# The root of a layer norm on VectorE, other waiting rules of the planner, and 40 buffers for 37

## The chip, the cores and the metric

The kernel runs on one core of a Trainium2 chip. The metric is the device time of one execution in microseconds (us). The core's engines work side by side and wait for one another by semaphores: TensorE (PE, matrix products and transposes; PEld is its loading of weights), VectorE (DVE), ScalarE (ACT), GpSimd (POOL), and SyncE (SP), which issues the loads and stores.

## The reference

Two layers over 256 tokens of 1024 features. Each layer is a feed-forward block, a mixer, and a feed-forward block, and each of the six ends in a layer norm over the residual:

```
for l in range(DEPTH):
    x = _layer_norm(DN_ALPHA * x + 0.5 * _swiglu(x, ...pre...), ln_pre_g[l], ln_pre_b[l])
    mix = _hybrid_mixer(x, ...) if l % 2 == 0 else _ssd_mixer(x, ...)
    x = _layer_norm(DN_ALPHA * x + mix, ln_mix_g[l], ln_mix_b[l])
    x = _layer_norm(DN_ALPHA * x + 0.5 * _swiglu(x, ...post...), ln_post_g[l], ln_post_b[l])

def _layer_norm(x, g, b):
    xc = x - mean(x, -1); var = mean(xc * xc, -1)
    return xc * rsqrt(var + 1e-5) * g + b

def _swiglu(x, w_gate, w_up, w_down):
    return (silu(x @ w_gate) * (x @ w_up)) @ w_down
```

The hybrid mixer joins a gated delta rule and an mLSTM in chunks of 64 tokens, the SSD mixer is a chunked state-space model; both begin and end with large products with weights. All of it is float32.

## The kernel before, in words

**Products.** TensorE multiplies in float32r. For the precision of float32 each operand is kept as two tiles, `hi` (rounded) and `lo` (the rest), and a product is three matmuls (`mm3`, L676): hi by hi, hi by lo, lo by hi. Six such matmuls are one group of the planner (`mm3k`, L683).

**Weights.** `_wload` (L538) brings half a weight block of some 0.5 MB at a time: a load on SyncE into `raw`, a cast on ScalarE (`hi`), a subtraction on VectorE (`lo = raw - hi`). All three, and most large tiles of the mixers, take a buffer from the tag `m4`, which has NSLOT = 37 slots (L33, L61).

**Stages.** Six stages follow each other: feed-forward, hybrid mixer, feed-forward, feed-forward, SSD mixer, feed-forward. A stage reads the normalized `x`, transposed and split into `xh` and `xl`. The 256 tokens are two halves of 128. `close` (L670) ends a stage: for each half the last products (`tail`), then `layer_norm`. So the second half's tail is there to cover the first half's norm, and the next stage's first products with the first half are there to cover the second half's norm. There are five borders between stages and one end.

**The layer norm** of one half (`_layer_norm`, L650) is on VectorE: for each of two blocks of 512 columns `x<-acc,x` adds the residual and `st` takes statistics; `mv` joins them to mean and variance; a pass `x<-x,mv,lng` for each block; a pass `x<-x,rr,lnb` for each block, which needs the reciprocal root `rr`. Then `x_transpose` (L598): eight transposes on TensorE (`tr`), casts on ScalarE (`xh`), subtractions on VectorE (`xl`). The root is `rsqrt1` (L621), five operations on GpSimd: `rv` = variance + eps, `ry` = its power -0.5, two operations for `rh` and one for `rr`, which are a Newton step.

**The order.** Nothing is executed in the order of the program text. `Plan` records all operations; `rank` (L313) gives each a due time, worked back from the order of TensorE's operations, in which those within `hp()` (L499, the layer norm among them) are dated 600 operations earlier; `order` (L344) then plays the engines through with the costs of `_cost` and writes down for each engine a fixed sequence. The chip's engines follow their sequences and wait for semaphores. In each step the planner takes, of the operations that could start, the one that is due first; one that becomes ready only `t - t0` later is preferred to one ready now if it is due earlier by more than WAIT times that, and if the time is under FRAC of the other one's busy time (L413). A GpSimd operation that uses the port shared with VectorE can start only at `dve_port`, the planned end of the last such VectorE operation, and the other way round:

```
if q == "DVE" and o.port:
    t = max(t, pool_end)
if q == "POOL" and o.port:
    t = max(t, dve_port)
```

A VectorE operation uses the port in the plan when none of its operands is in PSUM and it has more than one column (L292 of `_cost`, `op.port`). The planned end counts LAG (84 ns on VectorE) beyond the time at which the engine is free for its next operation, and a result reaches the next VectorE operation 35 ns after that (HAND).

Of the kernel before, what the change touches and what calls it, by code (L numbers as in the profile page):

```python
# [12 lines left out]
F32 = mybir.dt.float32  # L13
F32R = mybir.dt.float32r
I32 = mybir.dt.int32
AF = mybir.ActivationFunctionType
ALU = mybir.AluOpType
AX = mybir.AxisListType

P = 128  # L20
# [6 lines left out]
ALPHA = (2 * DEPTH) ** 0.25  # L27
LN_EPS = 1e-5
# [1 line left out]
BIG = 1e30  # L30
CW = 260
WMAX = KB * CW
NSLOT = 37  # L33
RSQRT_MAGIC = 0x5F3759DF

C_NEG = 0
# [23 lines left out]

SB_SLOTS = {"m4": (NSLOT, WMAX), "m2": (6, 512), "m1": (6, 256), "tiny": (12, 16), "tiny96": (12, 96)}  # L61
PS_SLOTS = {"acc": 4, "gu": 2, "tr": 2}
# [119 lines left out]
class Plan:  # L182
# [83 lines left out]
    def _cost(self, op, method, a, k):  # L266
        q = op.engines[0]
        out = a[0]
        n = out.cols if isinstance(out, View) else 0
        if q == "PE":  # L270
            if method == "transpose":
                op.busy += 112
            else:
                load = 110 * a[1].cols / 128
                if a[1].dtype == F32R:
                    op.busy += max(load, .4375 * a[2].cols + 6)
                else:
                    op.busy += 2 * max(load, .834 * a[2].cols)
        elif q == "SP":
            op.busy = 330  # L280
            src = a[1]
            shape = out.shape if isinstance(out, View) else src.shape
            op.bytes = 4 * math.prod(shape)
            op.small = not (isinstance(src, bass.AP) and src.tensor.name.startswith("in_w") or "raw" in getattr(getattr(out, "buf", None), "name", ""))
        else:
            ins = [v for v in list(a[1:]) + list(k.values()) if isinstance(v, View)]
            wide = [v for v in ins if v.cols > 1]
            n = max([n] + [v.cols for v in wide])
            scal = sum(v.cols == 1 for v in ins) if n > 1 else 0
            ps = any(v.buf.psum for v in ins + [out])  # L290
            if q == "DVE":
                op.port = not ps and n > 1  # L292
                if method == "reciprocal":
                    t = 150 + 6.3 * n
                elif method == "tensor_tensor_scan":
                    t = 150 + 2 * n
                elif len(wide) < 2 and method.startswith("tensor_") and not ps:
                    t = 150 + .52 * n + 60 * scal
                else:
                    t = 150 + 1.045 * n + 50 * scal  # L300
                op.busy += t - LAG["DVE"]
            elif q == "ACT":
                op.busy += 180 + .85 * n + 60 * scal - LAG["ACT"] + (186 if "accum_out" in k else 0)
                f = a[2] if method == "activation" and len(a) > 2 else None
                if f in EXPS:
                    op.exps = True
                elif f == AF.Silu:
                    op.exps = False
            else:
                op.port = method != "memset"  # L310
                op.busy += 100 + .85 * n if method == "memset" else 930 if k.get("op") == ALU.pow else 250 + 2.25 * n
# [27 lines left out]
            o.prio = due[o]  # L339

    PE_DUE = False
    WAIT, FRAC = 2, .25

    def order(self):  # L344
        ops = self.ops
# [12 lines left out]
        free = {t: [(0.0, i) for i in range(SB_SLOTS[t][0] if t in SB_SLOTS else PS_SLOTS[t])] for t in line}  # L358
# [10 lines left out]
        def offer(o):  # L369
            for q in o.engines:  # L370
                cand[q].append(o)
# [5 lines left out]
        def start(o, q):  # L377
            t = max(ready[o, q], clock[q])
            if o.news:
                need = collections.Counter()  # L380
                for b in o.news:
                    if b.tag in line:
                        k = need[b.tag]
                        need[b.tag] += 1
                        before = 0
                        for e in line[b.tag]:
                            if e is b:
                                break
                            before += 1
                        if len(free[b.tag]) <= before:  # L390
                            return None
                        t = max(t, sorted(free[b.tag])[k][0])
            if q == "DVE" and o.port:
# [3 lines that stand above are left out]
            return t  # L397

        def switch(o, q):
            return 1300 if q == "ACT" and o.exps is not None and o.exps != table else 0  # L400

        while len(out) < len(ops):
            best = None
            for q in QUEUES:
                can = [(t, o) for o in cand[q] for t in (start(o, q),) if t is not None]
                if not can:
                    continue
                t0 = max(min(t for t, _ in can), clock[q] + 1)
                now = [(o.prio + 2 * switch(o, q), o.n, t, o) for t, o in can if t <= t0]
                mine = min(now)  # L410
                for p, n, t, o in sorted((o.prio + 2 * switch(o, q), o.n, t, o) for t, o in can if t > t0):

                    if p + self.WAIT * (t - t0) < mine[0] and t - t0 < self.FRAC * mine[3].busy:  # L413
                        mine = (p, n, t, o)
                        break
                mine = (None, mine[2] + switch(mine[3], q), mine[3])
                if mine and (best is None or mine[1] < best[0]):
                    best = (mine[1], q, mine[2])
            if best is None:
                raise RuntimeError("no operation can start: " + str([(q, [(o.n, o.calls[0][0], [(b.name, b.tag, line[b.tag][0].name if line.get(b.tag) else None, len(free.get(b.tag, ()))) for b in o.news]) for o in c[:4]]) for q, c in cand.items() if c]))  # L420
            t, q, o = best
            for e in o.engines:
                cand[e].remove(o)
            busy = o.busy
            if q == "POOL" and len(o.engines) > 1:
                busy = 150 + (o.busy - 66) * 2.2
            for b in o.news:
                if b.tag in line:
                    line[b.tag].remove(b)
                    s = min(free[b.tag])  # L430
                    free[b.tag].remove(s)
                    b.slot = s[1]
                    held[b] = 0.0
            clock[q] = t + busy
            end = t + busy + LAG[q]
            if q == "SP":
                first = max(dma, t + busy)
                dma = first + o.bytes / (200 if o.small else 410)
                end = dma + 2000
            if q == "ACT" and o.exps is not None:  # L440
                table = o.exps
            if o.port and q == "POOL":
                pool_end = end
            if o.port and q == "DVE":
                dve_port = end
            o.done, o.begun, o.on = end, t, q
            out.append(o)
            for u in users[o]:
                for e in u.engines:
                    r = t + 1 if o in u.after else end + HAND[q][e]  # L450
                    ready[u, e] = max(ready[u, e], r)
                left[u] -= 1
                if not left[u]:
                    offer(u)
            touched = {v.buf for _, a, k in o.calls for v in list(a) + list(k.values()) if isinstance(v, View)}
            for b in sorted(touched, key=lambda b: b.n):
                b.left -= 1
                if b in held:
                    held[b] = max(held[b], end + 60)
                    if not b.left:  # L460
                        free[b.tag].append((held.pop(b), b.slot))
# [18 lines left out]
class Net:  # L480
# [140 lines left out]
    def rsqrt1(self, v, eps, scale=None):  # L621
# [13 lines left out]
        G.tensor_mul(r, y, h)  # L635
        return r

    def ln_load(self, g, b):
        nc = self.nc
        gt = self.m4([P, D], nm="lng")  # L640
        bt = self.m4([P, D], nm="lnb")
        nc.sync.dma_start(gt, g.partition_broadcast(P))
        nc.sync.dma_start(bt, b.partition_broadcast(P))
        return gt, bt
# [5 lines left out]
    def _layer_norm(self, half, accs, scale, gb, last):  # L650
        nc = self.nc
        t = self.x[:, half, :]
# [4 lines left out]
            nc.vector.bn_stats(st[:, n, :], t[:, sl])  # L657
        mv = self.tiny([P, 2], nm="mv")
        nc.vector.bn_aggr(mv, st)
        r = self.rsqrt1(mv[:, 1:2], LN_EPS / ALPHA ** 2)  # L660
        for n in range(2):
            sl = slice(n * 512, n * 512 + 512)
            nc.vector.scalar_tensor_tensor(t[:, sl], t[:, sl], mv[:, 0:1], gb[0][:, sl], op0=ALU.subtract, op1=ALU.mult)
# [933 lines left out]
```

## Time and profile before

| what | us |
| --- | --- |
| median of 3 runs | 1186.47 (1184.49 to 1188.71) |
| the profiled execution | 1190.74 |
| its span, first to last instruction | 1189.0 |
| TensorE busy | 1132.2 |
| VectorE busy | 755.5 |
| ScalarE busy | 567.1 |
| GpSimd busy | 54.7 |

The profile is of one execution. A row of a table of stretches gives the busy time of an engine in the stretch, the number of its instructions in brackets, the granted TensorE clock as a share of full speed, the share of the DMA engines and GB/s. A row in order of time gives start, length, engine, line and operation, what it writes and reads with shapes and count, and in square brackets how long the engine was idle just before and what ended that. All operations stand under one line of the program, that of `emit`, so they are told apart by the names of their tiles.

### The profile page before, as it was taken

The page shows a single profiled execution, that of the slowest core. Times are in us where ns is not written, and L with a number is a line of the kernel's source. Part 1 is how long each engine was busy: PE and PEld are TensorE (multiplying, and loading weights), DVE is VectorE, ACT ScalarE, POOL GpSimd, SP SyncE. Part 2 cuts the span into 40 slices and gives each one's busy share as a digit, 9 for nine tenths or more (in the row PEclk, how much of TensorE's full clock was granted, in tenths as well). Part 3 has the DMA queues.
Part 4 walks back from the last instruction along what each step waited for, and adds up shares of the span by engine and source line. Part 5 has one row for each costly group of instructions (what it writes and reads, how often), then busy time and mean ns, then how long its engine had stood idle before and what let it go on. Part 6 is the DMA issues. An engine that isn't in the chain of part 4 may idle for free. (4 is left out here: it accounts for less than half of the span.)

```text
span 1189.0 us, 19681 instructions
## 1 busy us (share of the span) xinstructions
PE 1132.2 (95%) x8052; PEld 1051.8 (88%) x8052; DVE 755.5 (64%) x1208; ACT 567.1 (48%) x808; POOL 54.7 (5%) x113
## 2 busy tenths in 40 slices
PE   6999999898996999999899999899999997999996
PEld 6999998898985999999799999789999877999995
DVE  6745556698858744545854435578999866544534
ACT  6636453474423444534343434358778444443420
POOL 0000002000001000000100000010011100000001
PEclk9999999999998999999999999999999998999999
DMA  9656554657335454566454656355455654555510
GB/s 365 222 185 211 202 201 139 184 164 234 107 105 166 144 197 161 194 204 202 145 195 152 197 170 226 127 184 196 142 158 168 204 174 176 178 202 179 209 61 36
DMA packets 75811, 210.02 MB, mean 177 GB/s; under 512 B 13564, under 2 KB 26056, under 8 KB 75720
## 3 DMA queue, kind: packets, MB, share of 16 engines
q1 hardware_dynamic: 75720, 208.76, 52.6%
q8 instruction: 63, 1.03, 0.3%
q14 instruction: 28, 0.23, 0.1%
HBM read 204.23 MB, written 4.50 MB: 176 GB/s over the span
## 5 line engine op out<-in xcount | busy, mean ns | idle before, releaser
L477 DVE TENSOR_TENSOR lo<-raw,hi 128x1024 fp32r<-128x1024 f32 (+1 forms) x356 | 431.3, 1223 | 278.8 <-ACT hi L477 275.4
L477 ACT CAST hi<-raw 128x1024 fp32r<-128x1024 f32 (+1 forms) x356 | 370.8, 1049 | 356.9 <-DMA raw<-in_wgu 214.3
L477 PE MATMUL gu<-xh,hi 128*128 128x256 f32 x1216 | 342.0, 281 | 3.5 <-DVE hf L477 3.5
L477 PE MATMUL gu<-xh,lo 128*128 128x256 f32 x1216 | 342.1, 281 | 0.0
L477 PE MATMUL gu<-xl,hi 128*128 128x256 f32 x1216 | 342.1, 281 | 0.0
L477 PEld LDWEIGHTS gu<-xh,hi 128*128 128x128 f32 x1216 | 229.7, 189 | 5.1 <-DVE hf L477 3.7
L477 PEld LDWEIGHTS gu<-xl,hi 128*128 128x128 f32 x1216 | 229.7, 189 | 1.4
L477 PEld LDWEIGHTS gu<-xh,lo 128*128 128x128 f32 x1216 | 229.6, 189 | 0.0
L477 PE MATMUL acc<-hi,h 128*128 128x512 f32 x704 | 227.0, 395 | 0.0
L477 PEld LDWEIGHTS acc<-hi,h 128*128 128x128 f32 x704 | 132.1, 188 | 29.7 <-ACT h L477 0.4
L477 PE MATMUL acc<-lo,h 128*128 128x512 f32 x352 | 138.5, 394 | 0.0
L477 PE MATMUL acc<-xh,hi 128*128 128x256 f32 x320 | 93.9, 293 | 0.0
L477 PE MATMUL acc<-xl,hi 128*128 128x256 f32 x320 | 90.2, 282 | 0.0
L477 PE MATMUL acc<-xh,lo 128*128 128x256 f32 x320 | 90.1, 281 | 0.0
L477 PEld LDWEIGHTS acc<-lo,h 128*128 128x128 f32 x352 | 66.1, 188 | 14.0
L477 DVE TENSOR_TENSOR hf<-sg,gu 128x256 f32<-128x256 f32 (+1 forms) x100 | 38.4, 384 | 45.3 <-ACT sg L477 45.2
L477 ACT ACTIVATE sg<-gu 128x256 f32<-128x256 f32 (+1 forms) x100 | 35.4, 354 | 66.1 <-PE gu L477 65.8
L477 PE MATMUL acc<-hi,xl 128*128 128x260 f32 x224 | 64.4, 288 | 2.4 <-DVE xl L477 2.4
L477 PE MATMUL acc<-hi,xh 128*128 128x260 f32 x224 | 65.1, 291 | 0.5 <-ACT xh L477 0.5
L477 PE MATMUL acc<-lo,xh 128*128 128x260 f32 x224 | 64.2, 287 | 0.0
L477 PEld LDWEIGHTS acc<-xh,hi 128*128 128x128 f32 x320 | 60.7, 190 | 1.2 <-issue 0.7
L477 PEld LDWEIGHTS acc<-xl,hi 128*128 128x128 f32 x320 | 60.6, 189 | 0.7 <-issue 0.7
(267 smaller groups left out, 1439.6 us busy)
## 6 DMA issues: line engine op xcount, KB each, us to landing
raw<-in_wgu SPq DMA_DIRECT2D x176, 512.0 KB, 5.7
raw<-in_wd SPq DMA_DIRECT2D x88, 512.0 KB, 4.0
raw<-in_ssd_fm SPq DMA_DIRECT2D x24, 512.0 KB, 4.8
raw<-in_ssd_tm SPq DMA_DIRECT2D x16, 520.0 KB, 5.3
raw<-in_hyb_fm SPq DMA_DIRECT2D x16, 512.0 KB, 3.9
raw<-in_ssd_out SPq DMA_DIRECT2D x16, 512.0 KB, 4.8
raw<-in_hyb_tm SPq DMA_DIRECT2D x12, 520.0 KB, 4.8
raw<-in_hyb_out SPq DMA_DIRECT2D x8, 512.0 KB, 5.3
```

The source lines that it names most:

```text
L477: getattr(engines[o.on], method)(*map(real, a), **{x: real(v) for x, v in k.items()})
```

## The change

The root of the layer norms is computed by a new `rsqrt_dve` on VectorE, in nine operations on tiles of 128x1: the sum with eps (scaled), two integer operations for a first guess, three Newton steps of two operations each. The SSD mixer keeps `rsqrt1`. FRAC of the planner, .25 for all engines, becomes a table: .5 for VectorE, ScalarE and GpSimd, 0 for TensorE and SyncE, which then never wait for an operation that is due earlier. The planner's price of a float32r matmul is fitted anew (118.0 ns for 256 columns by either, 231.7 for 230.0 for 512). NSLOT goes from 37 to 40, and the space of SBUF set aside for DMA descriptors is made 512 bytes a partition. The loop that counts free slots is only left earlier.

```
-NSLOT = 37
+NSLOT = 40

-                    op.busy += max(load, .4375 * a[2].cols + 6)
+                    op.busy += max(load, .4441 * a[2].cols + 4.3)

-    WAIT, FRAC = 2, .25
+    WAIT = 2
+    FRAC = {"PE": 0, "DVE": .5, "ACT": .5, "POOL": .5, "SP": 0}

-                if p + self.WAIT * (t - t0) < mine[0] and t - t0 < self.FRAC * mine[3].busy:
+                if p + self.WAIT * (t - t0) < mine[0] and t - t0 < self.FRAC[q] * mine[3].busy:

+    def rsqrt_dve(self, v, eps):
+        V = self.nc.vector
+        T = lambda n, dt=F32: self.tiny([P, 1], dt, n)
+        ve, q, i, y = T("rv"), T("rq"), T("ri", I32), T("ry")
+        V.tensor_scalar(ve, v, eps, 2.0 ** 26, op0=ALU.add, op1=ALU.mult)
+        V.tensor_scalar(i, ve.bitcast(I32), 1, None, op0=ALU.logical_shift_right)
+        V.tensor_scalar(y.bitcast(I32), i, -1, RSQRT_MAGIC - 2 ** 31, op0=ALU.mult, op1=ALU.add)
+        for c in (3.0, 12.0, 768.0):
+            V.tensor_scalar(q, ve, y, y, op0=ALU.mult, op1=ALU.mult)
+            V.scalar_tensor_tensor(y, q, -c, y, op0=ALU.add, op1=ALU.mult)
+        return y

-        r = self.rsqrt1(mv[:, 1:2], LN_EPS / ALPHA ** 2)
+        r = self.rsqrt_dve(mv[:, 1:2], LN_EPS / ALPHA ** 2)

-    nc = bacc.Bacc("TRN2", target_bir_lowering=False, num_devices=1)
+    nc = bacc.Bacc("TRN2", target_bir_lowering=False, num_devices=1, dynamic_dma_scratch_size=512)
```

## Rows read from the trace of the kernel before

**Rows 1.** The page's first part: busy us, share of span, instructions by engine.
```profile
PE 1132.2 (95%) x8052; PEld 1051.8 (88%) x8052; DVE 755.5 (64%) x1208; ACT 567.1 (48%) x808; POOL 54.7 (5%) x113
```

**Rows 2.** Waits of TensorE over the span: total, times, longest.
```profile
PE tr L477 <- DVE x L477: 11.8, 4, 4.8
...
PE gu L477 <- DVE hf L477: 5.1, 2, 3.5
```

**Rows 3.** TensorE in the stretches of borders 1, 2, 3, about 745, borders 4, 5.
```profile
205.00:220.00 15.00, 11.12 (x80) 0.89 0.52 144
380.00:400.00 20.00, 15.99 (x106) 0.91 0.41 132
575.00:597.00 22.00, 18.30 (x121) 0.92 0.56 191
744.00:756.00 12.00, 8.51 (x60) 0.86 0.36 124
775.00:797.00 22.00, 19.12 (x126) 0.92 0.55 191
984.00:1006.00 22.00, 14.97 (x106) 0.84 0.30 107
```

**Rows 4.** TensorE in two single microseconds after border 3's first wait.
```profile
583.00:584.00 1.00, 1.00 (x6) 0.50 1.03 422
...
586.00:587.00 1.00, 1.00 (x10) 0.96 0.00 0
```

**Rows 5.** VectorE in order of time at border 3.
```profile
574.32 0.69 DVE L477 SCALAR_TENSOR_TENSOR x<-acc,x 128x512 f32<-128x512 f32 x1 [1.05 <-PE acc L477]
...
575.77 1.23 DVE L477 TENSOR_TENSOR lo<-raw,hi 128x1024 fp32r<-128x1024 f32 x1
...
579.93 0.21 DVE L477 BATCH_NORM_AGGREGATE mv<-st 128x2 f32<-128x12 f32 x1
580.18 1.41 DVE L477 SCALAR_TENSOR_TENSOR x<-x,mv,lng 128x512 f32<-128x512 f32 x2
581.51 1.28 DVE L477 TENSOR_TENSOR xl<-tr,xh 128x512 fp32r<-128x512 f32 x2
583.54 3.77 DVE L477 TENSOR_TENSOR lo<-raw,hi 128x1024 fp32r<-128x1024 f32 x3 [0.75 <-ACT hi L477]
...
587.42 3.49 DVE L477 TENSOR_TENSOR lo<-raw,hi 128x1024 fp32r<-128x1024 f32 x3
...
591.43 0.75 DVE L477 SCALAR_TENSOR_TENSOR x<-x,rr,lnb 128x512 f32<-128x512 f32 x1
```

**Rows 6.** GpSimd at border 3, the last of its five operations.
```profile
582.82 0.19 POOL L477 TENSOR_TENSOR rr<-ry,rh 128x1 f32<-128x1 f32 x1
```

**Rows 7.** GpSimd's last operation and VectorE's pass at border 5.
```profile
986.69 0.19 POOL L477 TENSOR_TENSOR rr<-ry,rh 128x1 f32<-128x1 f32 x1
...
996.64 1.41 DVE L477 SCALAR_TENSOR_TENSOR x<-x,rr,lnb 128x512 f32<-128x512 f32 x2
```

**Rows 8.** A root on VectorE in the hybrid mixer, first and twelfth operation.
```profile
365.17 0.17 DVE L477 TENSOR_SCALAR ri<-oss 128x8 int32<-128x8 int32 x1
...
367.39 0.17 DVE L477 TENSOR_TENSOR of<-ry,rq 128x8 f32<-128x8 f32 x1
```

**Rows 9.** VectorE busy in border 2's stretch and in the SSD mixer.
```profile
380.00:400.00 20.00, 18.91 (x26) 0.91 0.41 132
...
800.00:900.00 100.00, 91.78 (x193) 1.00 0.54 174
```

**Rows 10.** VectorE in the last layer norm.
```profile
1181.62 1.41 DVE L477 SCALAR_TENSOR_TENSOR x<-x,mv,lng 128x512 f32<-128x512 f32 x2
1184.49 1.42 DVE L477 SCALAR_TENSOR_TENSOR x<-x,rr,lnb 128x512 f32<-128x512 f32 x2 [1.46 <-POOL rr L477]
```

**Rows 11.** VectorE at border 2, between the first half's statistics and its root.
```profile
381.32 1.22 DVE L477 TENSOR_TENSOR lo<-raw,hi 128x1024 fp32r<-128x1024 f32 x1
```

**Rows 12.** ScalarE about 745.
```profile
746.06 1.06 ACT L477 CAST hi<-raw 128x1040 fp32r<-128x1040 f32 x1 [2.29 <-DMA raw<-in_ssd_tm]
```

More of the change, by code (lines that the diff above doesn't have):

```diff
@@ L385, in start @@
                         before = 0
+                        room = len(free[b.tag])
                         for e in line[b.tag]:
-                            if e is b:
+                            if e is b or before >= room:
                                 break
                             before += 1
-                        if len(free[b.tag]) <= before:
+                        if room <= before:
                             return None
```

## The prediction, on record before the result

> **What bounds the kernel now.** I read the shares first, then the list of what TensorE waited for, then tables of the stretches where it waited, then VectorE's order there. TensorE is busy for 1132.2 of 1189.0 us [rows 1], so time can come only out of its idle 56.8 us and out of what it runs at the lower clock. Of its waits the largest is for `x`, 11.8 us in four waits, by the transposes that open a stage [rows 2]. Two waits for `hf` come to 5.1 us.
>
> The five borders between stages stand in [rows 3], which I number in order of time: idle 3.9, 4.0, 3.7, 2.9 and 7.0 us, 21.5 us together. Each also shows a mean granted clock of 0.84 to 0.92. Single microseconds of border 3 show what that is: after a wait the engine is fully busy at a granted 0.50, the lower of its two levels (1.2 and 2.4 GHz), and some 3 us later it has the upper one again [rows 4]. (1 - 0.89) x 15 = 1.65 us is lost that way at border 1, and 1.8, 1.75 and 1.75 at borders 2, 3 and 4. At border 5 it is 3.5, of which I take 2.5, since part of that low clock falls into idle time.
>
> Why does TensorE wait? Border 3 on VectorE: the statistics `mv` of the second half are done at 580.14 [rows 5], GpSimd has the root `rr` at 583.01 [rows 6], but the pass that uses it (`x<-x,rr,lnb`) starts at 591.43 [rows 5]. In the 8.4 us between, VectorE runs six weight subtractions `lo`. They stand ahead of it in its queue, which is fixed by the program. The same shows at all five borders; the longest is border 5, with `rr` at 986.88 and the pass at 996.64 [rows 7]. So GpSimd isn't slow; the written order is wrong, and the code says why. The planner starts a GpSimd operation only after the last VectorE operation that shares the port with it has ended (L395), and counts 84 ns more for that end than for VectorE's next start. While subtractions are there, the five GpSimd steps starve in the plan, one coming in wherever VectorE has a gap or touches PSUM, and the pass is written behind the subtractions. On the chip the steps ran at once.
>
> **The root on VectorE, per layer norm.** Five GpSimd operations go, nine VectorE operations of 128x1 come. No row shows this size; the nearest are the existing root's operations on 128x8. From its first operation to the next operation after it there are eleven intervals in 367.39 - 365.17 = 2.22 us, 0.202 each [rows 8]. Nine cost 1.82 us. The bounds: 1.5 if only their busy time counted (0.17 each, [rows 8]), and 2.2 if each took as long as the `mv` operation (0.21, [rows 5]) and the same gap. I take 1.82, from the rows that are the same arithmetic. GpSimd took 2.87 us from `mv` to `rr`.
>
> The steps are VectorE's own now, so L395 no longer applies to them. A subtraction would have to get into the gap between two steps, 119 ns in the plan (84 of lag, 35 of hand-over); `hp()` dates the steps 600 operations earlier, and FRAC of .5 (before .25) of a subtraction's 1.14 us in the plan covers that gap. So the second half's `x` is done 1.82 + 4 x 0.71 = 4.7 us after `mv` (two passes take 1.41, [rows 10]): at border 3 at 584.8, if nothing comes between, against 592.8.
>
> **Borders 1, 3, 4, 5.** TensorE has the first half's matmuls to run meanwhile: at border 3 from the `xl` of 581.51 to the pass of 591.43 [rows 5], about 10 us. With `x` 6 to 9 us earlier the second wait is covered. The first wait at borders 3 and 4 is another thing, one for `xl` of the first half, which VectorE runs behind the second half's `mv` and its passes [rows 5]. Today the first half's `x` is late there through a subtraction of 1.23 us in front of its pass with `rr` [rows 5], and VectorE idles for 1.05 us before the second half's first accumulator [rows 5]. Out go these 2.28 us, in come 1.82: the pass ends some 0.4 us earlier, and its `xl` comes before the second half's last accumulator is read, not after. I leave 0.5 us of wait at each of these three borders. Gains: border 1 3.9 + 1.65 - 0.5 = 5.0; border 3 3.7 + 1.75 - 0.5 = 5.0; border 4 2.9 + 1.75 - 0.5 = 4.1. At border 5 the shorter of the two waits for `hf` (5.1 together, the longer 3.5, [rows 2]) stays, so 7.0 - 1.6 + 2.5 = 7.9. Sum 22.0.
>
> **Border 2** goes the other way. The tail is short there, both halves' statistics meet on VectorE, which is busy for 18.9 of 20 us [rows 9]. The first half's pass with `rr` already waits behind the second half's reads and statistics. One subtraction in front of it (1.22 us, [rows 11]) goes, nine steps (1.82) come, and some five steps of the second half (1.0) get in as well: 1.6 us later. The first half's `xl` has a planner's priority just behind the second half's first pass with `rr`, so one more pass (0.7) gets in front. Loss 2.5 us, between 0 and 4.
>
> The Trainium skill ("VectorE: DVE Perf Modes", Rules for kernel authors) says of chained VectorE operations to minimize their count. By that the change is wrong wherever VectorE is the late engine; border 2 is the place where that agrees with the trace, at the others VectorE's subtractions have time to spare. The same page (The TRN2 errata) gives about 150 cycles at 0.96 GHz as the fixed cost, an estimate of 1.41 us for nine and, at border 2 and the end, 0.8 us less in the sum; the rows' 1.82 decides.
>
> **The end.** The last layer norm has no subtraction before it. There GpSimd's root ran beside two passes of 1.41 us together, and the pass with `rr` follows 2.87 us after their start [rows 10]; now all is in one queue, 1.82 + 1.41 = 3.23. Loss 0.35, between 0 and 0.8.
>
> **The rest.** VectorE gets 12 x 1.82 = 22 us more, 755.5 [rows 1] to 777, 65% of the span: hidden except as said. FRAC of .5 for VectorE and ScalarE puts steps of the mixers ahead of a subtraction or cast by up to 0.57 us; of 0 for TensorE and SyncE a transpose or load no longer holds its engine idle, and may come one group of six matmuls (0.7 us) later. The new matmul price differs by 0.01 us at most. I cost these at nothing: TensorE's other idle time, 56.8 less 21.5 less some 18 at the start and the end, about 17 us, may go either way by some 6 us. Three more slots are one half weight (`raw`, `hi`, `lo`) more in flight. It pays where casts wait for a load: at 745 TensorE lost 3.5 us idle and 1.7 of clock [rows 3] with ScalarE's `hi` waiting 2.29 us for a load [rows 12]. I leave that out of the sum and put it in the range. The smaller scratch has no user in this trace: all loads of the page are issued on SyncE; nothing.
>
> **Sum.** -22.0 + 2.5 + 0.35 = -19.1 us. The profiled execution took 1190.74 us, 1.74 above its span, and stands 4.3 above the median of 1186.47. Taken off the profiled one it gives 1171.6; off the median 1167.4, which I forecast. A measurement of this kernel can tell about 0.3%, 3.6 us, from no change.
>
> **Rivals.** (a) *The first half's `xl` is left behind the second half's steps* at borders 1, 3 and 4 as well, if it becomes ready after `mv`. It would start 1.82 + 3 x 0.71 = 4.0 us after `mv`, not 1.4 [rows 5]: 2.6 more wait at borders 3 and 4, about 2.2 at border 1, clock loss stays. Gains become 1.1, -1.3, -2.1 and 7.9, less 2.85: 2.8 us, so 1184. For it: the planner's priorities. Against: in the plan as in [rows 5] the first half's `x` precedes the second half's last read by a little. Chance 0.13. (b) *Waits behind late loads go too*: 745 (5.2 us), the `hf` of border 5 (1.6), and border 2 without loss (2.5): 1158. For it one half weight more ahead; against, the plan counts with it too. Chance 0.15. (c) *The subtractions become late*, slower. VectorE is 91.8% busy from 800 to 900 [rows 9], and up to 0.57 us of waiting in front of a subtraction uses up the 8.2 us of slack at the fifteenth; I take 5 us lost. At the borders six subtractions go behind 4.7 us of layer norm; TensorE waits from the point at which a subtraction ends after its matmul is due, at most 4.7 at each of five, 23 us. Against the 22 gained: 1186 + 5 + 23 - 19 = 1195. Against it: no wait for `lo` is among TensorE's larger ones [rows 2], so there is a lead today. Chance 0.08. (d) *It doesn't do what it says*: other subtractions still stand ahead of the pass, or the wait moves to `hf` and weights: 1186. Chance 0.07. The forecast has 0.57.
>
> **Range and chances.** The forecast's own unknowns (border 2 by 2.5, small waits and mixers by 6, the steps by 0.4 at six places) give 1160 to 1177. To leave out no more than 2 in 10 it reaches to (b), less 3 of the mixers, at 1155 and to (a) at 1184. Faster: 0.57 + 0.15 + 0.06 of (a) = 0.78; within 0.3%: the other 0.07 of (a) and 0.05 of (d), 0.12; slower: (c) and 0.02 of (d), 0.10.
>
> **What would show it.** Right: at the borders the pass with `rr` starts within 3.5 us after `mv`, the wait of the transposes for `x` falls from 11.8 to under 4 us, TensorE's idle in these stretches from 21.5 to 8 or less, with its clock at 0.97 or more at borders 1, 3, 4; border 2 is worse; the last pass starts 3.2 us after `mv`. Wrong: TensorE waiting for `xl` over 2 us at borders 3 and 4 (a), waiting for `lo`, or VectorE over 95% from 800 to 900 (c), subtractions still ahead of the pass (d).

## The result and the profile after

The changed kernel takes 1157.26 us (median of 4 runs, 1153.92 to 1159.14) against 1187.59 for the kernel before: ratio 0.9741, 95% interval 0.9705 to 0.9778, or 30 us less. The forecast was 1167.4, 19.1 less, with 1155 to 1184. The profiled execution after took 1153.92 us with a span of 1152.1; it is the shortest of its four and the profiled one of before was on the long side, so the two traces differ by 36.9 us of span, more than the medians do.

First the page: the engines' shares, which answer [rows 1].

```profile
PE 1116.6 (97%) x8052; PEld 1040.2 (90%) x8052; DVE 775.4 (67%) x1316; ACT 571.9 (50%) x810; POOL 23.7 (2%) x53
```

TensorE idles for 35.5 us, 21.3 less than before. VectorE has 19.9 us more work. Then TensorE's waits, total, times and longest, as in [rows 2]:

```profile
PE tr L479 <- DVE x L479: 7.7, 7, 5.9
PE tr L479 <- DVE md L479: 3.5, 2, 2.6
PE tr L479 <- DVE xl L479: 1.7, 1, 1.7
PE tr L479 <- DVE hf L479: 1.1, 2, 0.8
```

5.9 of the 7.7 for `x` is one wait, at border 2; six others share 1.8. The stretches that answer [rows 3], placed by the `mv` of the second half: border 1, border 2 with the end of the mixer, border 3, the place that was at 745, borders 4 and 5.

```profile
205.00:220.00 15.00, 14.71 (x124) 1.00 0.73 224
350.00:395.00 45.00, 37.89 (x249) 0.92 0.48 154
563.00:585.00 22.00, 19.87 (x156) 1.00 0.62 205
732.00:744.00 12.00, 12.00 (x92) 1.00 0.50 166
755.00:777.00 22.00, 21.69 (x171) 1.00 0.65 222
957.00:979.00 22.00, 21.75 (x183) 1.00 0.57 201
```

The clock stays at its upper level at borders 1, 3, 4 and 5. To see border 2 whole, this is the same stretch of the kernel before, with the wait of the mixer in it:

```profile
355.00:400.00 45.00, 34.99 (x196) 0.89 0.45 148
```

Idle time plus the time lost by the clock, (1 - clock) x length, before less after:

| place | before | after | gain | forecast |
| --- | --- | --- | --- | --- |
| border 1 | 5.5 | 0.3 | 5.2 | 5.0 |
| border 2 and the mixer's end | 15.0 | 10.7 | 4.3 | -2.5 |
| border 3 | 5.5 | 2.1 | 3.4 | 5.0 |
| about 745 | 5.2 | 0 | 5.2 | left out |
| border 4 | 4.6 | 0.3 | 4.3 | 4.1 |
| border 5 | 9.5 | 0.3 | 9.2 | 7.9 |
| end, after the last `mv` | 7.6 | 7.9 | -0.3 | -0.35 |

(For border 5 the clock loss of before is taken as 2.5, as in the forecast. At border 2 part of the low clock falls into idle time too, more of it after than before, so its gain is about 1 us too small here. The last row is plain time from the start of the last `mv` to the end of the span.) These are 31.3 of the 36.9 us; I did not follow the rest place by place.

What the steps look like: VectorE at border 4 after, in order of time. Before, the pass stood 9.6 us behind `mv` here (790.18 after 780.54).

```profile
760.29 0.21 DVE L479 BATCH_NORM_AGGREGATE mv<-st 128x2 f32<-128x12 f32 x1
760.53 0.15 DVE L479 TENSOR_SCALAR rv<-mv 128x1 f32<-128x1 f32 x1
...
761.10 0.27 DVE L479 TENSOR_SCALAR rq<-rv,ry 128x1 f32<-128x1 f32 x1
761.28 0.75 DVE L479 SCALAR_TENSOR_TENSOR x<-x,mv,lng 128x512 f32<-128x512 f32 x1
761.95 0.15 DVE L479 SCALAR_TENSOR_TENSOR ry<-rq,ry 128x1 f32<-128x1 f32 x1
...
762.95 0.16 DVE L479 SCALAR_TENSOR_TENSOR ry<-rq,ry 128x1 f32<-128x1 f32 x1
763.14 0.75 DVE L479 SCALAR_TENSOR_TENSOR x<-x,ry,lnb 128x512 f32<-128x512 f32 x1
```

The pass starts 2.64 us after `mv`, with no subtraction between. And the end, for [rows 10]: first step at 1144.47, pass at 1147.62, 3.15 us, where GpSimd's way took 2.87.

```profile
1144.47 0.15 DVE L479 TENSOR_SCALAR rv<-mv 128x1 f32<-128x1 f32 x1
...
1147.62 1.41 DVE L479 SCALAR_TENSOR_TENSOR x<-x,ry,lnb 128x512 f32<-128x512 f32 x2
```

### The profile page after: what moved, and what is told of

Same layout as the page of the kernel before. It is cut to its first block, busy times and chain, and to the rows that moved or that the text cites. A ratio compares the mean times of both kernels' runs of the same rounds, so it can differ in the third digit from the quotient of the medians.

```text
span 1152.1 us, 19730 instructions
## 1 busy us (share of the span) xinstructions
PE 1116.6 (97%) x8052; PEld 1040.2 (90%) x8052; DVE 775.4 (67%) x1316; ACT 571.9 (50%) x810; POOL 23.7 (2%) x53
## 4 chain that ended last, share of the span: by engine, by line
PE 83%; DVE 11%; DMA 3%; ACT 2%; issue 1%; SPq 0%; DVEq 0%; ACTq 0%
PE gu L479 45%; PE acc L479 34%; PE tr L479 4%; DVE x L479 3%; DVE lo L479 2%; DVE cv L479 1%; DMA raw<-in_wgu 1%; DVE st L479 1%; DVE rq L479 1%; DMA raw<-in_wd 1%; DMA ident<-in_ident 1%; ACT cv L479 1%; DVE ry L479 1%; DMA raw<-in_hyb_out 0%; DVE y L479 0%
## 5 line engine op out<-in xcount | busy, mean ns | idle before, releaser
L479 ACT CAST hi<-raw 128x1024 fp32r<-128x1024 f32 (+1 forms) x356 | 370.4, 1049 | 283.9 <-DMA raw<-in_wgu 149.2
L479 ACT CAST h<-hf 128x256 fp32r<-128x256 f32 x76 | 30.9, 406 | 76.0 <-DVE hf L479 76.0
```

What stands on the lines that cost most here:

```text
L479: getattr(engines[o.on], method)(*map(real, a), **{x: real(v) for x, v in k.items()})
```

## The experiments

Ratios are to the kernel before, of runs on the same chip, with 95% intervals.

**The root alone, and the order alone.** Three theories: the written order (the plan starved GpSimd's steps), the engine (GpSimd's root itself is slow), or FRAC and the slots.

```
e1: -        r = self.rsqrt1(mv[:, 1:2], LN_EPS / ALPHA ** 2)
    +        r = self.rsqrt_dve(mv[:, 1:2], LN_EPS / ALPHA ** 2)
e2: -                op.port = method != "memset"
    +                op.port = method != "memset" and n > 1
```

(e1 also takes in the new function `rsqrt_dve` itself.)

> The kernel before with the layer norms' roots on VectorE alone (FRAC .25 for all engines, 37 slots). Theory 1, the written order (the plan starved the GpSimd steps, so the passes with the root stood behind weight subtractions): 15 to 25 us faster than before, the pass with the root starts 2.5 to 3.5 us after mv at the borders, TensorE's wait of the transposes for x under 4 us. Theory 2, the engine (the root itself was slow on GpSimd): about 1 us a border, 5 us faster. Theory 3, most of the 30 us measured comes from FRAC and the slots: under 10 us faster.

> The kernel before, roots on GpSimd, with one rule of the plan changed: a GpSimd operation on one column doesn't wait for VectorE's port in the plan. No operation is changed, only the written order. Theory 1 (order): as much as the root on VectorE alone, 15 to 25 us faster, with GpSimd's five steps as long as before (2.9 us from mv to the root). Theory 2 (engine): no change, within 3 us.

e1: 0.9804 (0.9772 to 0.9837), 23 us. The pass comes 2.65 us after `mv` at borders 1, 3, 4 and 5, and 4.16 at border 2; the transposes still wait 5.4 us for `x` (with the waits put down to steps of the root), where I had expected under 4. e2: 0.9887 (0.9833 to 0.9942), 13.5 us, without any operation changed; one of its four executions stands 10 us over the other three. So the order is a cause by itself: theory 2 (no change by e2, 5 us by e1) falls. But on the old FRAC the order alone gave about 60% of e1, less than I expected of it. e2 at border 4, on VectorE and on GpSimd:

```profile
774.75 0.21 DVE L477 BATCH_NORM_AGGREGATE mv<-st 128x2 f32<-128x12 f32 x1
...
777.73 0.19 DVE L477 TENSOR_TENSOR sdt<-acc,svec 128x32 f32<-128x32 f32 x1 [1.32 <-ACT zs L477]
777.84 1.22 DVE L477 TENSOR_TENSOR lo<-raw,hi 128x1024 fp32r<-128x1024 f32 x1
778.97 1.41 DVE L477 SCALAR_TENSOR_TENSOR x<-x,rr,lnb 128x512 f32<-128x512 f32 x2
```

```profile
777.64 0.19 POOL L477 TENSOR_TENSOR rr<-ry,rh 128x1 f32<-128x1 f32 x1
```

Four us from `mv` to the pass, not 9.6; the root still takes 2.87, and one subtraction still stands in front. At border 1 of e2 nothing was won:

```profile
205.00:220.00 15.00, 11.56 (x85) 0.89 0.49 142
```

There an `hgate` that waits 3.20 us for a copy on ScalarE, and a subtraction, were written ahead of the pass.

```profile
207.53 0.18 DVE L477 TENSOR_TENSOR hgate<-acc,hgb 128x24 f32<-128x24 f32 x1 [3.20 <-ACT mv L477]
...
208.77 1.41 DVE L477 SCALAR_TENSOR_TENSOR x<-x,rr,lnb 128x512 f32<-128x512 f32 x2
```

**The order, with the rest of the change.** The same rule in the changed kernel, with the layer norms' roots back on GpSimd (e6), and with them on VectorE, so that only the SSD mixer's roots are freed (e7).

```
e6: -        r = self.rsqrt_dve(mv[:, 1:2], LN_EPS / ALPHA ** 2)
    +        r = self.rsqrt1(mv[:, 1:2], LN_EPS / ALPHA ** 2)
e6, e7: -                op.port = method != "memset"
        +                op.port = method != "memset" and n > 1
```

> The changed kernel (FRAC, 40 slots) with the roots back on GpSimd, and the plan's port rule not applied to one-column operations there. If the written order were all, as fast as the changed kernel (ratio 0.974). By the sum of the single runs (0.9887 for this order on the kernel before, 0.9963 and 0.9967 for FRAC and slots): 0.982.

> The changed kernel with the plan's port rule not applied to one-column GpSimd operations; that leaves the eight roots of the SSD mixer to be planned as early as they can run. If the starving in the plan costs there too: 2 to 5 us faster than the changed kernel. If TensorE has other work there (it idled 1.3 us from 800 to 950): no change, ratio 0.974 by 0.004.

e6: 0.9750 (0.9723 to 0.9776), the same as the change. With FRAC and the slots, GpSimd's root in the right order is as good as VectorE's: which engine computes the root makes no difference that these runs can tell. TensorE waits less for `x` there than in the changed kernel, partly because at border 2 it waits for the mixer's `gyl` (2.55 us) instead:

```profile
PE tr L479 <- DVE x L479: 3.9, 6, 1.4
```

e7: 0.9748 (0.9721 to 0.9776): nothing left to win at the SSD mixer's roots.

**FRAC, slots and price alone.**

> The kernel before with the new table FRAC alone. Theory 1: the borders stay as they are, 4 us faster to 4 slower. Theory 3: 10 us faster or more.

> The kernel before with 40 slots and the smaller descriptor space alone. Theory 1: the borders stay, at most the wait near 745 goes (5 us faster), 0 to 6 us faster. Theory 3: 10 us faster or more.

> The kernel before with the new matmul price alone: a change of 0 to 1.7 ns a matmul in the plan. It shows how much any reshuffling of the order moves the time. Expected within 4 us of before; if it moves by more, the 4 us of FRAC and of the slots are no more than reshuffling.

e3: 0.9963 (0.9943 to 0.9982). e4: 0.9967 (0.9947 to 0.9987). e8: 0.9998 (0.9978 to 1.0018). FRAC and the slots give some 4 us each by themselves and theory 3 falls; the new price gives none that can be measured. Multiplied, 0.9804 x 0.9963 x 0.9967 = 0.974, what the whole change gives, but by chance: the borders of e3 and e4 stay late, and the wait of 745 is gone in both (TensorE is busy throughout from 735 to 765 in e3 and from 730 to 760 in e4), a gain that can be had only once; and what border 2 gains is in neither.

**FRAC and slots taken out of the change.**

```
e9:  -    FRAC = {"PE": 0, "DVE": .5, "ACT": .5, "POOL": .5, "SP": 0}
     +    FRAC = {"PE": .25, "DVE": .25, "ACT": .25, "POOL": .25, "SP": .25}
e10: -NSLOT = 40
     +NSLOT = 37
     (and the descriptor space as before)
e11: -    FRAC = {"PE": 0, "DVE": .5, "ACT": .5, "POOL": .5, "SP": 0}
     +    FRAC = {"PE": .25, "DVE": .5, "ACT": .5, "POOL": .5, "SP": .25}
```

> The changed kernel with FRAC at .25 for all engines again (root on VectorE, 40 slots and the price stay). If the parts add up: 0.9804 x 0.9967 = 0.977, 4 us slower than the changed kernel. If FRAC is what brings the first half's layer norm at border 2 in front of the mixer's last products: the two mv of border 2 stand 5 to 6 us apart again (13.9 in the changed kernel, 5.5 with the root alone) and TensorE idles some 4 us in two waits there, 6 us slower, 0.979.

> The changed kernel with 37 slots and the descriptor space as before. If the parts add up: 4 us slower, ratio 0.977, with waits of ScalarE's casts for loads up by some 50 us in total and one wait of 3 us near 740 for hf. If the slots only matter where the borders are late: no change, 0.974.

> The changed kernel with FRAC .25 for TensorE and SyncE and .5 for the others. If VectorE's .5 (steps ahead of subtractions) is what moves border 2: as fast as the changed kernel, 0.974, the two mv there 12 us apart or more. If it is TensorE's 0: as with .25 for all engines, 0.977 to 0.979.

e9: 0.9806 (0.9781 to 0.9831). FRAC is worth 7 to 8 us within the change, and its place is border 2 with the mixer's end. TensorE there in e1, e9 and e11:

```profile
350.00:406.00 56.00, 44.05 (x268) 0.91 0.43 150
```

```profile
350.00:406.00 56.00, 44.53 (x278) 0.91 0.43 154
```

```profile
350.00:395.00 45.00, 38.25 (x244) 0.92 0.43 153
```

Idle and clock loss are 17.0 in e1 and 16.5 in e9, against 15.0 before: the root alone makes border 2 worse, by 2; in both, 1.9 of the loss are two waits for `hf` at 401 to 405, just behind the border. In e11 idle and clock loss are 10.4, as in the changed kernel, and e11 takes 0.9716 (0.9691 to 0.9741): it is the .5 of VectorE, ScalarE and GpSimd that does it (these three were not taken apart), and TensorE's and SyncE's 0 isn't needed.

The mechanism is in VectorE's order at the mixer's end. `gyl` is the low part of the mixer's output of the first half, which that half's last products read. `oss<-sq` opens the root of the second half's output, at the end of which stands its `o`. Before and after:

```profile
363.85 0.68 DVE L477 TENSOR_REDUCE oss<-sq 128x8 f32<-128x512 f32 x1
...
368.93 0.68 DVE L477 TENSOR_TENSOR gyl<-tr,gyh 128x512 fp32r<-128x512 f32 x1
```

```profile
357.25 0.68 DVE L479 TENSOR_TENSOR gyl<-tr,gyh 128x512 fp32r<-128x512 f32 x1
358.03 0.69 DVE L479 TENSOR_REDUCE oss<-sq 128x8 f32<-128x512 f32 x1
```

Before, `gyl` stands behind that whole root; after, ahead of it. So in all eight traces with VectorE's .5 (e3, e5, e6, e7, e10, e11, e12 and the change), and in none of the six with .25. TensorE then runs the first half's products while VectorE is at the second half's root, transposes the last `o` without a wait, and waits once, for the first half's `x`, where before it waited 5.25 us for `o`, then 2.92 and 0.69 for `x`:

```profile
369.16 1.09 PE L477 MATMUL tr<-ident,o 128*128 128x128 f32 x4 [5.25 <-DVE o L477]
```

```profile
363.33 0.63 PE L479 MATMUL tr<-ident,o 128*128 128x128 f32 x4
369.89 1.09 PE L479 MATMUL tr<-ident,x 128*128 128x128 f32 x4 [5.93 <-DVE x L479]
```

The two `mv` of border 2 show it too: they stand 13.9 us apart after (365.61 and 379.49), 14.6 in e11, 5.5 in e1 and e9. FRAC without the root in time (e3) has the same order and the two `mv` 11.8 us apart, and loses 18.8 there. With GpSimd's root freed in the plan (e6) the loss is 7.3. So at this border the parts don't add up: it takes FRAC and a root that is in time, on either engine.

e10: 0.9795 (0.9770 to 0.9820), 6 us slower than the change, though the two intervals overlap a little. The wait of 3 us near 740 that I had expected did not come back. The difference lies mostly in one place: in e10 a cast waited 8.1 us for its load in the hybrid mixer, held up ScalarE's next operation (`sg`, which TensorE waited for), and TensorE lost 7.6 idle and 5.2 by the clock in this stretch, against 3.5 and 1.8 in the changed kernel. First e10, then the change:

```profile
266.00:286.00 20.00, 12.44 (x87) 0.74 0.79 204
```

```profile
266.00:286.00 20.00, 16.52 (x126) 0.91 0.83 203
```

```profile
276.97 1.04 ACT L479 CAST hi<-raw 128x1024 fp32r<-128x1024 f32 x1 [8.11 <-DMA raw<-in_hyb_fm]
```

Between e1 (0.9804) and e9 (0.9806) the three slots and the price gave nothing. So what they are worth, 0 to 6 us, seems to hang on whether a late load meets ScalarE's order at a bad place; that rests on this one place. Casts' waits for the feed-forward's first weights fell from 214.3 to 149.2 us in the change, 173.9 in e10.

**How long the steps may be.**

```
e5:  +        for _ in range(9):
     +            V.tensor_scalar(y, y, 1.0, None, op0=ALU.mult)
e12: -        for c in (3.0, 12.0, 768.0):
     +        for c in (3.0, 12.0):
```

(e12 also scales by 2^8 and takes the positive first guess.)

> The changed kernel with nine more dependent operations of 128x1 behind each root (a multiplication by 1), 18 for 9: about 1.7 us more from mv to the pass in each of the 12 layer norms. If the steps at the borders are covered by the first half's matmuls, as forecast, only the end pays in full (1.7) and border 2 some more: 2 to 6 us slower than the changed kernel's 1157, ratio to before 0.976 to 0.980. If the root is on TensorE's path at every border: 6 x 1.7 = 10 us or more slower, ratio 0.983 or above.

> The changed kernel with two Newton steps for three, seven operations for nine (the root is then good to some 5e-6 and no better): 0.46 us less in each layer norm. If nine are covered at borders 1, 3, 4 and 5: 0.4 us at the end and up to 0.9 at border 2, no measurable change, 0.974. If each step still counts, as the doubled steps do (15 us for nine): 3 us faster, 0.971.

e5: 0.9883 (0.9855 to 0.9910), 17 us slower than the change, where I had expected 2 to 6. The transposes of the second half at border 4, in the changed kernel and in e5:

```profile
764.04 0.63 PE L479 MATMUL tr<-ident,x 128*128 128x128 f32 x4 [0.31 <-DVE x L479]
```

```profile
776.29 0.63 PE L479 MATMUL tr<-ident,x 128*128 128x128 f32 x4 [2.39 <-DVE x L479]
```

The wait is longer, and the low clock is back. That border in e5:

```profile
765.00:787.00 22.00, 18.97 (x129) 0.92 0.44 148
```

3.0 idle and 1.8 of clock, 4.5 more than the change for 1.7 us of steps. But this isn't the price of longer steps alone, for the order changed with them. In e5 the second of the first half's two `xl` was written behind the second half's `mv` (770.85), its steps and the first of its two passes with the root; in the change both stand ahead of `mv` (760.29). First e5, then the change:

```profile
768.81 0.68 DVE L479 TENSOR_TENSOR xl<-tr,xh 128x512 fp32r<-128x512 f32 x1
...
776.73 0.68 DVE L479 TENSOR_TENSOR xl<-tr,xh 128x512 fp32r<-128x512 f32 x1
```

```profile
757.65 1.28 DVE L479 TENSOR_TENSOR xl<-tr,xh 128x512 fp32r<-128x512 f32 x2
```

The same happened at borders 1 and 3. The first half's products that read that `xl` can't fill the wait, so the cover shrank while the steps grew, and e5 does not tell the two apart. Nor is the cover at its end at nine steps: behind the transposes of 764.04 the changed kernel still runs twelve matmuls of the first half (764.43 to 765.95; the second half's `xh` is cast at 765.49 at the earliest).

e12: 0.9694 (0.9661 to 0.9727), the shortest of all at 1154.71 us; its interval overlaps that of the change, and e11's in the same comparison is 0.9716, so that seven steps gain over nine isn't settled.

## Why the prediction was right, and where not

**What bounds.** Right: the time came out of TensorE's idle and low-clock time, 21.3 us of idle alone in the profiles.

**The cause at the borders.** Right, and shown: e2 changes nothing but the plan's rule and brings the pass forward, and e6, the change with GpSimd's root and that rule, is as fast as the change.

**Price of the root.** 1.82 forecast, bounds 1.5 to 2.2. At border 4 the pass starts 2.61 us after the first step, with one pass between that takes 0.67 to the next start, so 1.94; in e5, where no pass stands between, nine steps take 2.08 (771.09 to 773.17). The estimate was a little low because `rq`, with two per-partition scalars, takes 0.27; the others take 0.15.

**Borders 1, 4 and 5.** Right in place and nearly in size (5.2, 4.3 and 9.2 for 5.0, 4.1 and 7.9). The second wait is covered: the second half's transposes wait 0.25 to 0.40 us for `x` at borders 1, 3, 4 and 5. The first half's `xl` come ahead of the second half's last accumulator, as forecast (565.70 and 566.30 at border 3, the accumulator's read at 566.90). At border 5 the wait for `hf`, which I let stay, went too.

**Border 3.** Mis-sized: 3.4 for 5.0. The 0.5 us left over was 2.1 at full clock: 0.40 for `x`, as left, and 1.73 for an `xl` of the second half. The step that failed is "I leave 0.5 us of wait": it has no term for ScalarE, which casts `xh` before VectorE can take `xl`. There `xh` stood behind four casts of weights, the first two of which waited 2.55 and 0.81 us for their loads.

```profile
569.66 1.05 ACT L479 CAST hi<-raw 128x1024 fp32r<-128x1024 f32 x1 [2.55 <-DMA raw<-in_wgu]
...
574.96 0.58 ACT L479 CAST xh<-tr 128x512 fp32r<-128x512 f32 x1
```

```profile
575.57 0.69 DVE L479 TENSOR_TENSOR xl<-tr,xh 128x512 fp32r<-128x512 f32 x1 [1.84 <-ACT xh L479]
```

```profile
576.32 0.33 PE L479 MATMUL tr<-ident,hf 128*128 128x128 f32 x1 [1.73 <-DVE xl L479]
```

In e11, where those two loads came sooner (waits of 0.88 and 0.73), TensorE lost 0.18 at this place.

**Border 2.** Wrong in sign for the change. The step that failed is "I cost these at nothing", said of FRAC. I had priced what the .5 may do in one comparison (0.57 us) and not that it can move `gyl` ahead of the second half's root, and with it the first half's products and layer norm. That is 6.8 us between forecast and result, the largest single part. For the root alone the sign is right and the size, -2.0 in e1 for -2.5, is partly luck: the first half's pass stands 5.43 us after `mv` in e1 and 5.46 before, not 1.6 later, and TensorE's wait for it is 2.91 for 2.92; later came only `xl` (a wait of 1.10 for 0.13, where I had 0.7), and the two waits for `hf` behind the border were not in my sum.

**745.** Left out of the sum, put in rival (b): it went, 5.2 us. The slots alone remove it (e4, e9), and so does FRAC alone (e3, e10); e1 and e2, with neither, still have a wait for `hf` there (3.08 and 1.98 us).

**The end.** Right: 3.15 us for the 3.23 forecast.

**Rivals.** (a) did not come: after, TensorE's waits for `xl` are one of 1.7 us. (b) came by its number, 1158 by its sum against 1157, and only in part by its cause: of its three places 745 alone fits waits behind late loads, and there FRAC does as well as the slots; the wait for `hf` of border 5 is gone in e1 too, with 37 slots; and border 2 gained by FRAC. That the result lies in the range, 2 us from its lower end, is owed to (b), so in part to luck; the forecast itself was 10 us too slow. (c) did not: VectorE went from 91.8% to 95.7% busy from 800 to 900, above the line I had drawn for it, and TensorE did not wait for a subtraction. (d) did not. Of the signs of being right one failed besides "border 2 is worse": the transposes' wait for `x` fell to 7.7 us, not under 4, 5.9 of it at border 2.

What stays open: 5.6 of the 36.9 us between the traces; which engine's FRAC moves `gyl`; how many steps the borders cover with the order held; and whether fewer steps or e11's FRAC beat the change, for which the intervals are too wide.

## What to carry to other kernels

When an in-order engine runs a result's consumer long after the result was ready, look at what is written ahead of it before making the producer faster: with the rest of the change in place, correcting the planner's rule for one engine gave the same time as moving the work to another engine (e6). Idle time hidden under other work is not a fixed budget: making the hidden part longer is a way to measure the cover, but a planner may write another order for it, as in e5, so compare the two orders before reading the difference as the price. Parts of a change to a schedule can be worth something only together, as FRAC and the root at border 2, so take each out of the whole as well as putting it in alone.

## What the runs showed of the hardware

The cost of a small VectorE operation on 128x1 was 0.15 us without a per-partition scalar and 0.27 with two (`rq`, 36 in the trace, 0.265 to 0.275); no run has one with a single such scalar. From the start of a 0.15 us operation to that of the next, which needs its result, it was 0.19; from `rq` 0.31, and 0.18 where an independent pass came next.

A root on GpSimd ended 2.87 us after `mv` in eight of the twelve layer norms before, and 3.28 to 3.95 after it in the other four, where one of its operations on 128x1 took 0.81 to 1.41 us that took 0.34 or 0.19 in the rest.

The length of a wait did not decide TensorE's clock by itself. Behind 2.19 us at border 3 before (to 582.25) the granted clock was 0.66 from 582 to 587; behind 2.19 us at border 1 of e4 (to 205.68) it stayed 1.00 from 203 to 213, and behind 3.08 us in e1 (to 738.25) 1.00 from 735 to 750.
